# Two transformer blocks on one core: eight split chunks in output projections, row weights through GpSimd's queue, modulation on two engines

## The chip, the cores and the metric

The kernel runs on one core of a Trainium2 chip. The metric is the device time of one execution in microseconds (us). Times are medians of several runs; a profile is one execution more, with its own time.

## What is computed

Two transformer blocks in a row, on 512 tokens of width 1024, all in float32. Cut to what matters here:

```python
# first block: three residual steps, each  x = x + rms_norm(f(rms_norm(x, g_pre)), g_post)
mix = concat(fox_attention(...), chunked_rel_attention(...)) @ w_out
ca  = memory_cross_attention(h, m, w_mem_q, w_mem_kv, w_mem_o)
ff  = (silu(h @ w_gate) * (h @ w_up)) @ w_down

# second block, two layers (an mLSTM, then latent attention), each with
cond = silu(c)                                  # one vector of 1024
ada = cond @ ada_w[l] + ada_b[l]                # one row of 6 * 1024
sh1, sc1, g1, sh2, sc2, g2 = split(ada, 6)
h = rmsnorm(x, norm_g[l, 0]) * (1 + sc1) + sh1
y = mlstm_mixer(h, ...) if l == 0 else mla_mixer(h, ...)   # each ends in  @ w_out
x = x + g1 * rmsnorm(y, norm_g[l, 1])
h = rmsnorm(x, norm_g[l, 2]) * (1 + sc2) + sh2
x = x + g2 * rmsnorm(square(relu(h @ w1)) @ w2, norm_g[l, 3])
```

## The kernel before

Every float32 value that TensorE multiplies is held as two parts, high and low, and each product of 128 rows is three matmuls (L445, L446, L447: high by high, high by low, low by high). Weights are loaded raw on SP's queue (L421, four buffers), in chunks of up to 512 KB, and split on the chip: ScalarE writes the high part (L307, or L317 where a gain is multiplied in), VectorE the low part (L308, L318). At most `wcap` chunks are split and live at a time; `cap` sets that number for a stage: 4 for the first block's output projections, 5 for later ones. All split chunks and large activations lie in one pool of 14 buffers of 8 KB per partition.

Activations between stages are transposed and split too: `parts` makes the high part on ScalarE (L620) and the low part on VectorE (L621).

`out_lin` is an output projection (w_out, w_mem_o, a_w_out, b_w_out). It makes the first 512 columns for all four token tiles, and then, per token tile t, the other 512, followed by `boundary`. There the work of a token tile is a chain over four engines: ScalarE sums the squares of the product (L577), GpSimd makes the reciprocal root (`rstd`: L566, L560), VectorE multiplies by the gain row (L690) and adds to the residual (L641), ScalarE and GpSimd do the norm of the new residual (L577, L566, L560), ScalarE scales by it (L596), TensorE transposes (L606, in `put`), and `parts` follows (L620, L621). At three boundaries (before the mLSTM, and before the MLP of each layer of the second block) `put` also modulates: VectorE applies scale and shift to each of the eight 128x128 blocks of a token tile (L612), reading columns that `gcol` hands out.

These columns and the gain rows come from a background program, `ada`, a generator that is advanced one step at a time. `row_by` makes 512 numbers of a row: it loads eight pieces of the weights (L845, on SP's queue, two buffers `araw`), multiplies and adds them on VectorE (L841), folds the upper half of the partitions on the lower (L849), splits (L620, L621), sums over the partitions on TensorE (L858), finishes the row on VectorE (L871 or L875) and writes it to DRAM (L201). `row_cols` reads a whole row back as eight columns (L381), transposes it on TensorE (L385) and copies it (L387). Where the steps stand in the order of the work:

```python
    def step(self, cost):
        self.tick(cost)
        self.pace -= cost
        if self.pace < 0 and not self.quiet:
            self.pace = BUF["pacb" if self.late else "pace"]
            self.step_bg()

    def gcol(self, name):
        while name not in self.gcols:
            self.step_bg()
        return self.gcols[name]
```

`step` is called once per three matmuls with a cost of 0.65, so a step of the background is taken every 3 us of products (2.5 from the mLSTM on), and none in a boundary (`quiet`). Who calls `gcol` for columns that aren't there yet makes all missing steps on the spot. Instructions then go to the queues of the engines by a static order that the framework's scheduler works out at build time; each engine runs its queue in that order, and buffers of a pool are reused in it.

Of the kernel before, what the change touches and what calls it, by code (L numbers as in the profile page):

```python
# [10 lines left out]
F32 = mybir.dt.float32  # L11
# [3 lines left out]
AF = mybir.ActivationFunctionType  # L15
ALU = mybir.AluOpType
# [4 lines left out]
P = 128  # L21
# [3 lines left out]
KD = 8  # L25
# [5 lines left out]
D_FF = 2816  # L31
ALL = slice(0, S)

BUF = dict(s8=14, u2=17, row=2, raw=4, w0=4, w1=4, w2=4, w3=5, w4=5, w5=5, w6=5, w7=5, ps=8, pace=3, pacb=2.5, man=0, lag=3, lagx=3, lagm=3, half=1, quiet=1, xp=0, fp=2, r1=1.25, r1b=3.6, r1c=2.4, r2=1.6, r2b=2.6, rx=1.4, rm=0.6, pre=10, gl=3, pl=0, hb=300, hs=0, ha=0, sp=0, spq=1.3, sq=1, b1=1, b2=1, lc=7, mb=(6, 8, 6, 6, 6), mc=(4, 3, 4, 4, 4), st2=1, pr2=8, z1=4.5, z2=5, gt=3, rv=2, gs=1, rl=3, n1=4, ex=2, em=3, vg=1, sb=(8, 8, 6), mo=4, x1=2, g0=20, st=1, y1=0, y2=1, y3=0, ph=0, pq=0, fy=1, u1=6, s32=4, sm=60)

TWO_PI = 2.0 * np.pi

# [1 line left out]
def tt(t):  # L39
    return slice(t * P, (t + 1) * P)  # L40
# [98 lines left out]
class Net:  # L139
# [27 lines left out]
    def big(self, shape, dt=F32):  # L167
        return self.t("s8", shape, dt, BUF["s8"])

    def u2(self, shape=(P, S), dt=F32):  # L170
        if BUF["u1"] and int(np.prod(shape[1:])) <= 256:
            return self.t("u1", shape, dt, BUF["u1"])
        return self.t("u2", shape, dt, BUF["u2"])

    def row(self, n=DM):
        return self.t("row", [P, n], F32, BUF["row"])

    def sm(self, n=1, p=P, dt=F32):
        if n > 8:
            return self.t("sm32", [p, n], dt, BUF["s32"])  # L180
        return self.t("sm", [p, n], dt, BUF["sm"])
# [194 lines left out]
    def cols_steps(self, name, srcs, eng=None):  # L376
        n = sum(k for _, k in srcs)
        r = self.u2((n, P))
        o = 0
        for src, k in srcs:  # L380
            (eng or self.nc.gpsimd).dma_start(out=r[o:o + k, :], in_=src.rearrange("(k p) -> k p", p=P))  # L381
            o += k
        yield None
        ps = self.bank((P, n))
        self.nc.tensor.transpose(out=ps, in_=r, identity=self.ident[:n, :n])  # L385
        c = self.t(f"cols_{name}", [P, n], F32, 1)
        self.nc.vector.tensor_copy(out=c, in_=ps)  # L387
        yield c

    def gains(self):  # L390

        a = self.a
        names = (("out", "g_fox_out", 4), (None, "g_chunk_out", 4), ("mem", "g_mem_pre", 8), ("kvm", "g_mem_kv", 8),
                 ("ffn", "g_ffn_pre", 8), ("qlat", "b_q_latent_g_2", 3))
        srcs = [(a[m][0], n) for _, m, n in names]
        srcs += [(a["kv_latent_g_2"], 2), (a["a_head_g_2"][0].rearrange("h d -> (h d)"), 8)]
        steps = self.cols_steps("all", srcs)
        next(steps)
        yield
        gc = next(steps)  # L400
        o = 0
        for m, n in (("out", 8), ("mem", 8), ("kvm", 8), ("ffn", 8), ("qlat", 3), ("lat", 2), ("head", 8)):
            self.gcols[m] = gc[:, o:o + n]
            o += n
# [195 lines left out]
    def put(self, ys, h, k, t, mod=None):  # L600

        for y, cw in ys:
            n = cw // P
            ps = self.bank((P, n, P))
            for j in range(n):
                self.nc.tensor.transpose(out=ps[:, j, :], in_=y[:, tt(j)], identity=self.ident)  # L606
            hi, lo = h.blk(k, n, tt(t))
            if mod:
                g, sh = mod
                y = self.u2((P, n, P))  # L610
                for j in range(n):
                    self.nc.vector.tensor_scalar(out=y[:, j, :], in0=ps[:, j, :], scalar1=g[:, k + j:k + j + 1],  # L612
                                                 scalar2=sh[:, k + j:k + j + 1], op0=ALU.mult, op1=ALU.add)
                ps = y
            self.parts(hi, lo, ps)
            k += n
# [67 lines left out]

    def out_lin(self, w, h, g, nxt, first, gain=None):
        y0, s0 = [], []

        def by_gain(ps, c):
            y = self.u2()
            self.nc.vector.tensor_tensor(out=y, in0=ps, in1=g[:, c:c + S], op=ALU.mult)  # L690
            return y

        if self.started:
            wg, pss, k0 = self.started
            self.started = None
        else:
            wg, pss, k0 = self.weights(w, 0, KD, 0, S, gain=gain), [], 0
        for t in range(NT):
            ps = pss[t] if pss else self.bank()
            self.run(self.out_part(wg, ps, t, h, k0, KD))  # L700
            s0.append(self.meansq(ps, S, DM))
            y0.append(by_gain(ps, 0))
        wg = self.weights(w, 0, KD, S, S, gain=gain)

        def y_of(t):
            ps = self.bank()
            self.run(self.lin_N(ps, wg, t, h, last=t == NT - 1))
            ss = s0[t] + self.meansq(ps, S, DM)
            return (y0[t], by_gain(ps, S)), ss

        self.boundary(y_of, nxt, first)
# [115 lines left out]
    def row_by(self, i, c, ws, n, vec, b=None, gain=None, kind=0):  # L827

        nc, V = self.nc, self.nc.vector
        acc = self.u2((P, n))  # L830
        if b is not None:
            nc.gpsimd.memset(acc, 0.0)
            self.small(acc[0:1, :], b.rearrange("(o c) -> o c", o=1))
        yield
        raws = {}
        for k in range(0, KD + 2, 2):
            for j in (k, k + 1):
                if j == 2 and b is None:
                    V.tensor_scalar(out=acc, in0=raws.pop(0), scalar1=vec[:, 0:1], scalar2=None, op0=ALU.mult)
                elif j >= 2:  # L840
                    V.scalar_tensor_tensor(out=acc, in0=raws.pop(j - 2), scalar=vec[:, j - 2:j - 1], in1=acc,  # L841
                                           op0=ALU.mult, op1=ALU.add)
                if j < KD:
                    raws[j] = self.t("araw", [P, n], F32, 2)
                    nc.sync.dma_start(out=raws[j], in_=ws[:, j, :])  # L845
            yield
        if BUF["fy"]:
            h = P // 2
            (V if BUF["fy"] == 1 else nc.gpsimd).tensor_tensor(out=acc[0:h, :], in0=acc[0:h, :], in1=acc[h:P, :], op=ALU.add)  # L849
            hl = self.u2((P, n), F32R)  # L850
            for _ in range(BUF["y1"]):
                yield
            self.parts(hl[0:h, :], hl[h:P, :], acc[0:h, :])
            yield
            for _ in range(BUF["y2"]):
                yield
            ps = self.bank((P, n))
            nc.tensor.matmul(ps, lhsT=self.onesr, rhs=hl, start=True, stop=True)  # L858
        else:
            hi, lo = self.u2((P, n), F32R), self.u2((P, n), F32R)  # L860
            for _ in range(BUF["y1"]):
                yield
            self.parts(hi, lo, acc)
            yield
            for _ in range(BUF["y2"]):
                yield
            ps = self.bank((P, n))
            nc.tensor.matmul(ps, lhsT=self.onesr, rhs=hi, start=True, stop=False)
            nc.tensor.matmul(ps, lhsT=self.onesr, rhs=lo, start=False, stop=True)
        if gain is None:  # L870
            V.tensor_copy(out=acc[0:1, :], in_=ps[0:1, :])  # L871
        else:
            g = self.u2((1, n))
            self.small(g, gain.rearrange("(o c) -> o c", o=1))
            V.scalar_tensor_tensor(out=acc[0:1, :], in0=ps[0:1, :], scalar=1.0 if kind == 1 else 0.0,  # L875
                                   in1=g, op0=ALU.add, op1=ALU.mult)
        self.small(self.arow[i:i + 1, c:c + n], acc[0:1, :])
        if c or n < S:
            self.have.add(i)
        yield  # L880
# [1068 lines left out]
```

## Time and profile before

| | |
|---|---|
| runs | median 2008.97 us of 3 (2007.26 to 2010.29) |
| profiled execution | 2011.87 us |
| its span, first to last instruction | 2010.1 us |
| mean granted clock of TensorE | 0.987 |
| busy: TensorE, VectorE, ScalarE, GpSimd | 1947.1, 1283.3, 1022.9, 220.1 us |
| moved by DMA | 241.93 MB, 120 GB/s on average |

A row of the profile names the line of the kernel, the engine (PE is TensorE, PEld its weight loads, DVE VectorE, ACT ScalarE, POOL GpSimd, SP SyncE; a q behind a name is the engine's instruction queue), the operation, and out<-in by the program's names. An arrow in brackets names what ended the idle time ahead of the instruction.

### The profile page before, as it was taken

What the parts mean: (1) busy time and instruction counts of PE and PEld (TensorE: products, weight loads), DVE (VectorE), ACT (ScalarE), POOL (GpSimd) and SP (SyncE); (2) the same over time, 40 slices, a digit from 0 to 9 for tenths busy, and PEclk for the clock granted to TensorE, in tenths of its full rate; (3) what the DMA queues carried; (4) which work ended last, traced back from release to release, by engine and by line L of the source; (5) the groups of instructions that cost most, each with busy time, mean ns of one, the idle gap of its engine ahead of it and who ended that gap; (6) DMA issues with size and microseconds to landing.
All of it is one profiled execution on the core that took longest, in us unless ns stands there. A gap on an engine that the chain in (4) does not pass through costs nothing. (4 is left out here: it accounts for less than half of the span.)

```text
span 2010.1 us, 28210 instructions
## 1 busy us (share of the span) xinstructions
PE 1947.1 (97%) x10174; PEld 1647.7 (82%) x10174; DVE 1283.3 (64%) x2565; ACT 1022.9 (51%) x2236; POOL 220.1 (11%) x463
## 2 busy tenths in 40 slices
PE   8999998999999999998998999999999989999998
PEld 5888987878888888777887888887888879989987
DVE  5756654756657675667776556566669745757666
ACT  6767775537244333545545442442565645545444
POOL 1331111001000100111112000000120012000000
PEclk9999999999999999999998999999999999999999
DMA  6322342433446463235342446455243212233322
GB/s 211 90 79 67 113 139 72 144 109 97 146 147 199 153 193 110 76 111 157 102 134 88 137 148 209 147 181 184 66 129 120 70 51 71 82 106 118 99 75 83
DMA packets 190988, 241.93 MB, mean 120 GB/s; under 512 B 20107, under 2 KB 119584, under 8 KB 190848
## 3 DMA queue, kind: packets, MB, share of 16 engines
q1 hardware_dynamic: 185264, 232.15, 36.7%
q0 software_dynamic: 5584, 7.98, 1.5%
q8 instruction: 80, 1.31, 0.3%
q14 instruction: 60, 0.49, 0.1%
HBM read 237.88 MB, written 2.20 MB: 119 GB/s over the span
## 5 line engine op out<-in xcount | busy, mean ns | idle before, releaser
L445 PE MATMUL ps<-s,s 128*128 128x512 f32 (+4 forms) x2452 | 935.8, 384 | 33.1 <-ACT s L620 33.1
L446 PE MATMUL ps<-s,s 128*128 128x512 f32 (+5 forms) x2452 | 927.2, 379 | 1.5 <-DVE s L621 1.5
L447 PE MATMUL ps<-s,s 128*128 128x512 f32 (+5 forms) x2452 | 926.2, 379 | 2.4 <-DVE s L621 2.4
L445 PEld LDWEIGHTS ps<-s,s 128*128 128x128 f32 (+1 forms) x2452 | 464.4, 190 | 119.7 <-ACT s L620 36.1
L447 PEld LDWEIGHTS ps<-s,s 128*128 128x128 f32 (+2 forms) x2452 | 463.9, 189 | 92.7 <-DVE s L621 3.9
L446 PEld LDWEIGHTS ps<-s,s 128*128 128x128 f32 (+2 forms) x2452 | 465.0, 190 | 87.5 <-DVE s L621 2.7
L307 ACT ACTIVATE s<-raw 128x512 fp32r<-128x512 f32 x329 | 185.3, 621 | 179.2 <-PE ps L447 118.4
L308 DVE TENSOR_TENSOR s<-raw,s 128x512 fp32r<-128x512 f32 x329 | 212.0, 686 | 66.7 <-ACT s L307 65.2
L841 DVE SCALAR_TENSOR_TENSOR u<-araw,cond,u 128x512 f32<-128x512 f32 x224 | 168.2, 751 | 134.7 <-DMA araw<-in_ada_w 108.0
L317 ACT ACTIVATE s<-raw,cols_all 128x256 fp32r<-128x256 f32 (+1 forms) x305 | 143.1, 545 | 39.5 <-issue 19.1
L318 DVE SCALAR_TENSOR_TENSOR s<-raw,cols_all,s 128x256 fp32r<-128x256 f32 (+1 forms) x305 | 147.2, 537 | 16.4 <-ACT s L317 14.8
L508 PEld LDWEIGHTS ps<-s,s 128*128 128x128 f32 x1092 | 130.0, 189 | 1.0
L508 PE MATMUL ps<-s,s 128*128 128x256 f32 x1092 | 130.3, 280 | 0.0
L621 DVE TENSOR_TENSOR s<-u,s 128x512 fp32r<-128x512 f32 x118 | 80.6, 691 | 71.8 <-ACT s L620 67.2
L620 ACT ACTIVATE s<-u 128x512 fp32r<-128x512 f32 x118 | 73.5, 627 | 74.5 <-DVE u L1392 58.4
L201 POOL DMA_DIRECT2D arow<-u x30 | 14.7, 489 | 707.1 <-DVE u L875 401.7
L621 DVE TENSOR_TENSOR s<-ps,s 128x512 fp32r<-128x512 f32 (+3 forms) x100 | 59.4, 605 | 44.1 <-ACT s L620 43.2
L1427 ACT ACTIVATE u<-ps 128x512 f32<-128x512 f32 x38 | 22.6, 596 | 104.2 <-PE ps L447 104.1
L1332 DVE TENSOR_TENSOR u<-ps,u 128x512 f32<-128x512 f32 x80 | 53.5, 683 | 29.8 <-PE ps L447 29.4
L620 ACT ACTIVATE s<-ps 128x512 fp32r<-128x512 f32 (+3 forms) x100 | 51.5, 527 | 38.8 <-PE ps L606 12.4
L566 POOL TENSOR_SCALAR sm<-sm,sm 128x1 f32<-128x1 f32 x34 | 11.3, 332 | 495.4 <-ACT junk L577 494.8
L318 DVE SCALAR_TENSOR_TENSOR s<-raw,cols_mix,s 128x128 fp32r<-128x128 f32 (+2 forms) x152 | 52.4, 400 | 9.7 <-ACT s L317 9.4
(257 smaller groups left out, 1976.1 us busy)
## 6 DMA issues: line engine op xcount, KB each, us to landing
raw<-in_mlp_w SPq DMA_DIRECT2D x128, 512.0 KB, 4.0
araw<-in_ada_w SPq DMA_DIRECT2D x192, 256.0 KB, 3.0
raw<-in_w_gate_up SPq DMA_DIRECT2D x44, 512.0 KB, 4.2
raw<-in_w_in SPq DMA_DIRECT2D x24, 512.0 KB, 4.7
raw<-in_a_w_in SPq DMA_DIRECT2D x24, 512.0 KB, 3.8
raw<-in_w_down SPq DMA_DIRECT2D x22, 512.0 KB, 4.1
raw<-in_w_mem_kv SPq DMA_DIRECT2D x16, 512.0 KB, 3.5
araw<-in_kv_ada_w SPq DMA_DIRECT2D x32, 256.0 KB, 2.7
```

The costliest lines, as they stand in the source:

```text
L307: A.activation(hi[:, sl, cl], src[:, sl, cl], AF.Copy)
L308: f.tensor_tensor(out=lo[:, sl, cl], in0=src[:, sl, cl], in1=hi[:, sl, cl].bitcast(F32), op=ALU.subtract)
L317: A.activation(hi[:, i, :], src[:, i, :], AF.Copy, scale=g)
L318: V.scalar_tensor_tensor(out=lo[:, i, :], in0=src[:, i, :], scalar=g, in1=hi[:, i, :].bitcast(F32), op0=ALU.mult, op1=ALU.subtract)
L445: self.nc.tensor.matmul(ps, lhsT=ah, rhs=bh, start=first and i == 0, stop=False)
L446: self.nc.tensor.matmul(ps, lhsT=ah, rhs=bl, start=False, stop=False)
L447: self.nc.tensor.matmul(ps, lhsT=al, rhs=bh, start=False, stop=last and i == n - 1)
L508: nc.tensor.matmul(ps, lhsT=l[:, k, :], rhs=m[:, k, :], start=first and k == e == 0, stop=k == 3 and e == 2, skip_group_check=True)
L620: self.nc.scalar.activation(hi, x, AF.Copy)
L621: self.nc.vector.tensor_tensor(out=lo, in0=x, in1=hi.bitcast(F32), op=ALU.subtract)
L841: V.scalar_tensor_tensor(out=acc, in0=raws.pop(j - 2), scalar=vec[:, j - 2:j - 1], in1=acc, op0=ALU.mult, op1=ALU.add)
L1332: V.tensor_tensor(out=y, in0=ps, in1=y, op=ALU.add)
```

## The change

`out_lin` sets `wcap` to 8 for its stage. The pieces of row weights are loaded on GpSimd's queue instead of SP's, into four buffers instead of two, and each is multiplied two steps after its load instead of one, so that `row_by` has one step more (10 instead of 9). `cols_steps` waits three steps instead of one between the read-back and the transpose, so that `row_cols` has two more (4 instead of 2). In `put`, blocks 0 and 1 of every four are modulated on VectorE and blocks 2 and 3 on ScalarE. The pool of 2 KB buffers has 15 instead of 17.

```diff
-BUF = dict(s8=14, u2=17, ...
+BUF = dict(s8=14, u2=15, ..., oc=8, ar=4, ...
@@ cols_steps
-        yield None
+        for _ in range(3):
+            yield None
@@ gains
-        gc = next(steps)
+        for gc in steps:
+            pass
@@ put
-                    self.nc.vector.tensor_scalar(out=y[:, j, :], in0=ps[:, j, :], scalar1=g[:, k + j:k + j + 1],
-                                                 scalar2=sh[:, k + j:k + j + 1], op0=ALU.mult, op1=ALU.add)
+                    gj, sj = (c[:, k + j:k + j + 1] for c in (g, sh))
+                    if j < 2:
+                        self.nc.vector.tensor_scalar(out=y[:, j, :], in0=ps[:, j, :], scalar1=gj, scalar2=sj,
+                                                     op0=ALU.mult, op1=ALU.add)
+                    else:
+                        self.nc.scalar.activation(y[:, j, :], ps[:, j, :], AF.Identity, scale=gj, bias=sj)
@@ out_lin
         y0, s0 = [], []
+        self.cap(BUF["oc"], True)
@@ row_by
-        for k in range(0, KD + 2, 2):
+        for k in range(0, KD + 4, 2):
+            for j in (k - 4, k - 3):
+                if j == 0 and b is None:
+                    V.tensor_scalar(out=acc, in0=raws.pop(0), scalar1=vec[:, 0:1], scalar2=None, op0=ALU.mult)
+                elif j >= 0:
+                    V.scalar_tensor_tensor(out=acc, in0=raws.pop(j), scalar=vec[:, j:j + 1], in1=acc,
+                                           op0=ALU.mult, op1=ALU.add)
             for j in (k, k + 1):
-                if j == 2 and b is None:
-                    V.tensor_scalar(out=acc, in0=raws.pop(0), scalar1=vec[:, 0:1], scalar2=None, op0=ALU.mult)
-                elif j >= 2:
-                    V.scalar_tensor_tensor(out=acc, in0=raws.pop(j - 2), scalar=vec[:, j - 2:j - 1], in1=acc,
-                                           op0=ALU.mult, op1=ALU.add)
                 if j < KD:
-                    raws[j] = self.t("araw", [P, n], F32, 2)
-                    nc.sync.dma_start(out=raws[j], in_=ws[:, j, :])
+                    raws[j] = self.t("araw", [P, n], F32, BUF["ar"])
+                    nc.gpsimd.dma_start(out=raws[j], in_=ws[:, j, :])
             yield
```

How the order of the instructions changes is shown at three places. The changed kernel is a few lines longer, so its lines have other numbers: L386, L447 to L449, L598, L608, L626, L647, L848, L853, L857, L866, L883 and L579 are there what L385, L445 to L447, L596, L606, L620 (L627 for L621), L641, L841, L845, L849, L858, L875 and L577 are before.

TensorE at the boundary after b_w_out, before: ps_15370 is the second half of the product for token tile 1, ps_15417 for tile 2, ps_15490 for tile 3, and L606 transposes tile 0.

```order
L446 MATMUL ps_15370<-s_2956_15267,s_2878_14948 128x512
L447 MATMUL ps_15370<-s_2956_15267,s_2879_14949 128x512
L445 MATMUL ps_15417<-s_2869_14919,s_2717_14411 128x512
L446 MATMUL ps_15417<-s_2869_14919,s_2717_14411 128x512
...
L447 MATMUL ps_15417<-s_2956_15267,s_2879_14949 128x512
L606 MATMUL ps_15447<-ident_66,u_2987_15400 128x128 x4
L606 MATMUL ps_15460<-ident_66,u_2988_15402 128x128 x4
L445 MATMUL ps_15490<-s_2869_14919,s_2717_14411 128x512
```

The same place in the changed kernel: ps_15233 is the product for tile 1, ps_15367 for tile 2.

```order
L448 MATMUL ps_15233<-s_2903_15109,s_2825_14786 128x512
L449 MATMUL ps_15233<-s_2903_15109,s_2826_14787 128x512
L866 MATMUL ps_15302<-u_2953_15299,onesr_78 128x512
L866 MATMUL ps_15339<-u_2965_15336,onesr_78 128x512
L386 MATMUL ps_15347<-ident_66,u_2968_15345 128x8
L447 MATMUL ps_15367<-s_2816_14757,s_2663_14250 128x512
L608 MATMUL ps_15397<-ident_66,u_2940_15263 128x128 x4
L608 MATMUL ps_15410<-ident_66,u_2941_15265 128x128 x4
L448 MATMUL ps_15367<-s_2816_14757,s_2663_14250 128x512
```

Both partition sums of row 10 and the transpose of its columns now stand between the two products; before, the two sums stand about 960 and 590 instructions further ahead.

VectorE at the same place in the changed kernel, from the residual of tile 1 on (six products of each half of the row left out):

```order
L647 SCALAR_TENSOR_TENSOR x_9_90<-u_2939_15261,sm_15356,x_9_90 128x512
L848 SCALAR_TENSOR_TENSOR u_2944_15271<-araw_15274,cond_4066,u_2944_15271 128x512
...
L848 SCALAR_TENSOR_TENSOR u_2944_15271<-araw_15292,cond_4066,u_2944_15271 128x512
L857 TENSOR_TENSOR u_2944_15271<-u_2944_15271 64x512
L627 TENSOR_TENSOR u_2953_15299<-u_2944_15271,u_2953_15299 64x512
L883 SCALAR_TENSOR_TENSOR u_2944_15271<-ps_15302,u_2955_15304 1x512
L848 SCALAR_TENSOR_TENSOR u_2956_15308<-araw_15311,cond_4066,u_2956_15308 128x512
...
L848 SCALAR_TENSOR_TENSOR u_2956_15308<-araw_15329,cond_4066,u_2956_15308 128x512
L857 TENSOR_TENSOR u_2956_15308<-u_2956_15308 64x512
L627 TENSOR_TENSOR u_2965_15336<-u_2956_15308,u_2965_15336 64x512
L883 SCALAR_TENSOR_TENSOR u_2956_15308<-ps_15339,u_2967_15341 1x512
```

Before, the residual of tile 1 is followed by L690 of tile 2 and the modulation of tile 0, and no row product stands in the boundary.

ScalarE at the boundary after the first out_lin, before: s_800 and s_803 are the transposed activation, L317 splits the weights of the next product.

```order
L596 ACTIVATE u_806_3682<-x_9_90,sm_3630 128x512
L620 ACTIVATE s_803_3676<-ps_3671 128x4x128
L317 ACTIVATE s_814_3704<-raw_3496,cols_all_1926 128x256 x4
L317 ACTIVATE s_815_3713<-raw_3509,cols_all_1926 128x256 x2
L577 ACTIVATE junk_3691,sm_3690<-x_10_91 128x1024
L317 ACTIVATE s_815_3713<-raw_3509,cols_all_1926 128x256 x2
L317 ACTIVATE s_816_3722<-raw_3522,cols_all_1926 128x256 x4
L317 ACTIVATE s_817_3731<-raw_3535,cols_all_1926 128x256 x4
L620 ACTIVATE s_800_3667<-ps_3741 128x4x128
```

And in the changed kernel, where s_808 and s_811 are that activation:

```order
L598 ACTIVATE u_814_3726<-x_9_90,sm_3674 128x512
L626 ACTIVATE s_808_3711<-ps_3706 128x4x128
L579 ACTIVATE junk_3735,sm_3734<-x_10_91 128x1024
L626 ACTIVATE s_811_3720<-ps_3715 128x4x128
L317 ACTIVATE s_822_3748<-raw_3528,cols_all_1926 128x256 x4
L626 ACTIVATE s_808_3711<-ps_3785 128x4x128
```

Of the 16 splits that stood between the two token tiles' L620, four are left there.

## Rows read from the trace of the kernel before

**Rows 1.** The page, first part: busy us (share of the span) and instructions of each engine.

```profile
PE 1947.1 (97%) x10174; PEld 1647.7 (82%) x10174; DVE 1283.3 (64%) x2565; ACT 1022.9 (51%) x2236; POOL 220.1 (11%) x463
```

**Rows 2.** Waits of TensorE over the span: line, releaser, us, times, longest.

```profile
PE ps L445 <- ACT s L620: 33.1, 10, 8.3
PE ps L858 <- DVE u L621: 5.3, 1, 5.3
...
PE ps L385 <- DMA u<-arow: 3.1, 1, 3.1
```

**Rows 3.** Timeline, boundary after b_w_out, TensorE: start us, us, engine, line, operation.

```profile
1637.67 0.39 PE L445 MATMUL ps<-s,s 128*128 128x512 f32 x1
```

**Rows 4.** Timeline of VectorE: columns "10" ready, and the boundary after b_w_out.

```profile
1502.10 0.17 DVE L387 COPY cols<-ps 128x8 f32<-128x8 f32 x1 [0.30 <-PE ps L385]
...
1636.52 1.41 DVE L641 SCALAR_TENSOR_TENSOR x<-u,sm,x 128x512 f32<-128x512 f32 x2 [0.37 <-POOL sm L560]
...
1641.21 1.42 DVE L641 SCALAR_TENSOR_TENSOR x<-u,sm,x 128x512 f32<-128x512 f32 x2 [0.59 <-POOL sm L560]
...
1645.23 2.64 DVE L612 TENSOR_SCALAR u<-ps,cols,cols 128x128 f32<-128x128 f32 x8
```

**Rows 5.** VectorE's row products L841: a wait of theirs, us and times.

```profile
  DMA araw<-in_ada_w: 108.0, 83
```

**Rows 6.** Timeline of 903 to 920 us: SP's queue, VectorE, ScalarE, TensorE.

```profile
903.90 9.73 SPq L845 DMA_DIRECT2D araw<-in_kv_ada_w  x5
...
912.53 0.75 DVE L841 SCALAR_TENSOR_TENSOR u<-araw,cond,u 128x512 f32<-128x512 f32 x1
913.20 1.89 DVE L308 TENSOR_TENSOR s<-raw,s 128x512 fp32r<-128x512 f32 x3
915.11 0.69 DVE L849 TENSOR_TENSOR u<-u 64x512 f32<-64x512 f32 x1
...
915.83 0.63 ACT L620 ACTIVATE u<-u 64x512 fp32r<-64x512 f32 x1 [2.11 <-DVE u L849]
...
918.89 0.77 PE L858 MATMUL ps<-u,onesr 128*128 128x512 f32 x1 [5.25 <-DVE u L621]
```

**Rows 7.** The chain that ended last, at 1387 to 1394 us: start us, us, what.

```profile
1387.74 0.49 DMA arow<-u
...
1390.49 2.98 DMA u<-arow
...
1393.52 0.22 PE ps L385
```

**Rows 8.** DMA issues (KB each, median us to landing), and the spread of negG's landings.

```profile
araw<-in_ada_w SPq DMA_DIRECT2D x192, 256.0 KB, 3.0
...
u<-negG POOLq DMA_DIRECT2D x8, 256.0 KB, 3.7
...
arow<-u POOLq DMA_DIRECT2D x28, 2.0 KB, 2.0
...
u<-arow POOLq DMA_DIRECT2D x10, 4.0 KB, 1.7
...
DMA to landing us min/median/max: 1.8/3.7/5.8
```

**Rows 9.** Timeline of ScalarE at the boundary after the first out_lin.

```profile
330.50 2.50 ACT L317 ACTIVATE s<-raw,cols_all 128x256 fp32r<-128x256 f32 x6
...
333.94 4.09 ACT L317 ACTIVATE s<-raw,cols_all 128x256 fp32r<-128x256 f32 x10
337.93 0.58 ACT L620 ACTIVATE s<-ps 128x512 fp32r<-128x512 f32 x1
```

**Rows 10.** ScalarE: splits after b_w_out, and a form of L620 (ns min/median/max).

```profile
1648.44 4.26 ACT L307 ACTIVATE s<-raw 128x512 fp32r<-128x512 f32 x8
...
L620 ACT ACTIVATE u<-ps x20: 257/590/608, 1488.5 to 1585.7; 128x512 fp32r<-128x512 f32 x16, 128x128 fp32r<-128x128 f32 x4
```

**Rows 11.** Timeline of the start: TensorE's second matmul, tile 1's norm on GpSimd.

```profile
9.61 0.63 PE L446 MATMUL ps<-s,s 128*128 128x512 f32 x1
...
13.50 0.82 POOL L593 TENSOR_SCALAR u<-x,sm 128x512 f32<-128x512 f32 x1
```

**Rows 12.** Busy us by engine in one stretch; PEclk is the granted clock (1.00 is full).

```profile
916.00:923.00 7.00, 4.11 (x10) 3.31 (x11) 6.56 (x9) 3.60 (x9) 1.66 (x3) 0.53 0.46 144
```

More of the change, by code (lines that the diff above doesn't have):

```diff
@@ L32 @@
 ALL = slice(0, S)
-BUF = dict(s8=14, u2=17, row=2, raw=4, w0=4, w1=4, w2=4, w3=5, w4=5, w5=5, w6=5, w7=5, ps=8, pace=3, pacb=2.5, man=0, lag=3, lagx=3, lagm=3, half=1, quiet=1, xp=0, fp=2, r1=1.25, r1b=3.6, r1c=2.4, r2=1.6, r2b=2.6, rx=1.4, rm=0.6, pre=10, gl=3, pl=0, hb=300, hs=0, ha=0, sp=0, spq=1.3, sq=1, b1=1, b2=1, lc=7, mb=(6, 8, 6, 6, 6), mc=(4, 3, 4, 4, 4), st2=1, pr2=8, z1=4.5, z2=5, gt=3, rv=2, gs=1, rl=3, n1=4, ex=2, em=3, vg=1, sb=(8, 8, 6), mo=4, x1=2, g0=20, st=1, y1=0, y2=1, y3=0, ph=0, pq=0, fy=1, u1=6, s32=4, sm=60)
+BUF = dict(s8=14, u2=15, row=2, raw=4, w0=4, w1=4, w2=4, w3=5, w4=5, w5=5, w6=5, w7=5, ps=8, pace=3, pacb=2.5, man=0, lag=3, lagx=3, lagm=3, half=1, quiet=1, xp=0, fp=2, r1=1.25, r1b=3.6, r1c=2.4, r2=1.6, r2b=2.6, rx=1.4, rm=0.6, pre=10, gl=3, pl=0, hb=300, hs=0, ha=0, sp=0, spq=1.3, sq=1, b1=1, b2=1, lc=7, oc=8, ar=4, mb=(6, 8, 6, 6, 6), mc=(4, 3, 4, 4, 4), st2=1, pr2=8, z1=4.5, z2=5, gt=3, rv=2, gs=1, rl=3, n1=4, ex=2, em=3, vg=1, sb=(8, 8, 6), mo=4, x1=2, g0=20, st=1, y1=0, y2=1, y3=0, ph=0, pq=0, fy=1, u1=6, s32=4, sm=60)
 TWO_PI = 2.0 * np.pi
```

## The prediction

> **What bounds the kernel now.** I read the busy shares first: TensorE works 97% of the span [rows 1], so no arithmetic is taken away by this change and the time can only move through the pauses of TensorE and through its clock. The list of what TensorE waited for comes next [rows 2]: 33.1 us in ten waits of L445 for ScalarE's L620 (the high parts of an activation after a boundary, 8.3 us the longest), one wait of 5.3 us of L858, one of 3.1 us of L385 for a row read back from DRAM. All pauses together are 63 us (2010.1 less 1947.1). After a pause the granted clock falls too: in the stretch after the wait of L858 it was 0.53, the lower of the two levels [rows 12], and TensorE's work took twice as long there. So a pause costs its length plus some microseconds. Then, for the places where the change moves instructions, I read the timelines and the order.
>
> **The background grows by 50 steps, and one row comes late: the largest term.** row_by yields 10 times instead of 9 (30 calls: 30 steps), row_cols 4 times instead of 2 (10 calls: 20 steps). Steps are handed out at a fixed pace of TensorE's work (2.5 us in the second half), so 50 steps are at least 125 us of products, and more on the clock, since attention and boundaries hand out none. Before, the columns "10" (the scale of the boundary after b_w_out) were finished at 1502.1 us, and that boundary's first residual additions come some 135 us later [rows 4]: no room is left. The order shows the result: nxt's gcol("10") now forces the row inside the boundary. On TensorE, in order, the two L858 of row 10 and its L385 stand between token tile 1's product and tile 2's product; on VectorE all 16 products of row 10 stand behind tile 1's L641. Nothing that TensorE could do instead stands ahead of them.
>
> Its length, by rows: TensorE is free when tile 1's product ends, at 1637.7, and tile 1's L641 ends at 1641.21 + 1.42 = 1642.6 [rows 3, 4]: 4.9 us. Sixteen products L841 start 0.67 apart where nothing holds them (912.53 to 913.20 [rows 6]): 10.7 us. Two tails (L849 0.69, L620 0.63, then L621 and L875, which I take as long as L849, and L858 at full clock, half of its 0.77 [rows 6]) are about 3.1 each: 6.2 us. Writing the row to DRAM and reading it back took 5.8 us from issue to L385 in the one place where TensorE waited for it [rows 7]; with the medians of landing, 2.0 and 1.7, it is about 4 [rows 8]. The floor, with every weight already on the chip, is 4.9 + 10.7 + 6.2 + 4 = 26 us. The weights aren't all there: four buffers hold four of the 16 loads, so rounds two and four wait for a landing. A landing takes 3.0 us at the median from SP's queue; the nearest rows for 256 KB from GpSimd's queue are negG's, 1.8 at least, 3.7 at the median, 5.8 at most [rows 8]. A round of products covers 2.7 us of it, which leaves some 1.7 for each of two rounds, and a little for GpSimd's own instructions between (two issues, a memset, tile 1's rstd). I take 30 us (negG's median; between 26 and 36, the end with landings of 5.8 in every round). TensorE restarts at the lower clock and loses about 2.5 us more, as after L858's wait (4.1 us busy in that stretch at half speed [rows 12]). **+32.5 us, between 27 and 39.** The 7 us pause that stands behind this boundary today stays.
>
> **Row products two steps behind their loads.** Before, VectorE stood at L841 until the weight had landed, 108.0 us in 83 waits for in_ada_w alone [rows 5]. That hurts TensorE in one place: at 903.9 SP needed 9.73 us for five loads, VectorE's products and so L849, L621 and L858 came late, and TensorE idled 5.25 us [rows 6]. With four buffers and two steps of distance the wait goes: −5.25, and −2.1 of half clock: **−7.4** (−7.4 to −2, if half the pause stays). The rule of the Trainium skill, "DMA: Bandwidth & Descriptors", section "Issuing engines are not separate DMA queues", says that the queues of all engines feed the same 16 DMA engines and that a second queue saves only issue time. The trace speaks differently for this place: SP's queue lost its time to waiting for a buffer, not to issuing, with raw weights queued behind. By the rule alone this term would be near 0 and the sum 7 us higher.
>
> **Columns two more steps behind their read-back.** L385's wait of 3.1 us [rows 2, 7] goes, with about 1.7 of low clock after it: **−4.8** (−4.8 to 0).
>
> **Eight chunks in out_lin.** At the first out_lin ScalarE's order changes: today 16 splits L317 (6, then 10 in 4.09 us) stand ahead of tile 1's L620 at 337.93 [rows 9]; after, four do. Twelve splits at 0.41 are 4.9 us on ScalarE, the pause there is 3.6 us and its low clock some 1.7: **−4.5** (−6 to −2.5). At the memory, a_w_out and b_w_out boundaries the splits of the next weights that stand ahead of tile 1's norm and L620 are as many as before (16, 8 and 8; the eight take 4.26 us [rows 10]): they are of later chunks, which costs ScalarE the same. **0**: those pauses stay.
>
> **Half the modulation on ScalarE.** 48 of 96 L612 move. Eight take VectorE 2.64 us per token tile [rows 4], so VectorE gains 1.3. ScalarE gains four of 128x128 from PSUM, for which the nearest row is the shortest L620, 0.26 [rows 10]: some 1.1 us per token tile, on the engine whose eight splits, norm and L620 are the chain at this boundary. For tile 0 it fills a wait of ScalarE for L612; for tile 1 it is on the path, less VectorE's gain. **+0.5** at each of three boundaries, **+1.5** (0 to 4.5, with all of it on the path at each).
>
> **The start.** GpSimd now issues four weight loads (1 MB) ahead of the first rstd, and tile 1's transposes stand behind TensorE's second matmul instead of its 22nd. Today tile 1's norm is ready no earlier than 13.50 + 0.82 on GpSimd [rows 11], TensorE's second matmul starts at 9.6: a wait of some 4 us, part of which returns as a shorter wait for tile 3 at 25 us. **+3.3** (0 to 6, if tile 1's input lands later as well).
>
> **mLSTM.** GpSimd's queue now has the weight loads among its 256 KB loads of negG; a load that waits for a buffer holds what is behind it. No row prices it; I take **0**, within one landing: ±3.
>
> **The sum.** 32.5 − 7.4 − 4.8 − 4.5 + 1.5 + 3.3 = +20.6 us on the profiled execution, 2011.87 (a span of 2010.1 and 1.8 around it): 2032.5. That execution is 2.9 above the median of the runs, 2008.97, so I expect 2029.5. All low ends together give 2015, all high ends 2057; a measurement of this kernel can tell about 0.2%, 4 us.
>
> **Rivals.**
> A, not slower: the boundaries shrink instead. The mechanism is ScalarE at the boundaries: with eight chunks held, the splits are done during the previous product, and the ten waits for L620 go. Price: up to some 28 of the 33.1 us [rows 2] and about 12 of low clock behind them instead of my −4.5 + 1.5; 2029.5 − 37 = 1993. It breaks even where the boundaries give 24 us. Against it: the order keeps the splits ahead of L620 at all but one, and the forced row's 26 us has no way round in TensorE's order. Chance 0.13, for all degrees of it.
> B, GpSimd's queue is slow under VectorE's load: landings at negG's worst, 5.8 [rows 8], so the forced row costs 36, the pause at 913 stays, and GpSimd's rstd waits behind loads in mLSTM: 2029.5 + 6 + 7 + 3 = 2045. The Trainium skill has a rule for it, "SBUF — State Buffer", 'The "DVE blocks DMA" trap (SWDGE)': while VectorE runs certain two-port operations, GpSimd can't write its descriptors and its transfers stall. The spread of negG's landings allows it, no row shows it. Chance 0.17.
> C, the change does not do what it says: the eight chunks find no room in the pool even at the first out_lin. Then −4.5 falls away: 2034. Chance 0.1.
> My forecast, a net loss by the forced row: 0.6.
>
> **Numbers.** Range 2006 to 2046: it takes in forecast, B and C, and half of A. Slower 0.85 (all but A and a small part of the forecast's low end), same 0.07, faster 0.08.
>
> **What would show it.** TensorE's waits should have new rows, L858 for VectorE's L621 and L385 for the row's read-back, of some 30 us together near 1640 to 1670, with the clock low behind them; no wait at 913 and none of L385 at 1390; the pause at 335 under 2 us, those at 465, 1078 and 1651 as long as now, and a wait of L606 near 10 us. If TensorE has no wait above 10 us at the boundary after b_w_out, the prediction is wrong.

## The result and the profile after

The changed kernel takes 2039.08 us at the median of four runs (2038.71 to 2042.21), the kernel before 2009.63 in the same series (2007.26 to 2011.11): a ratio of 1.0151, with a 95% interval of 1.0134 to 1.0169. Slower, as forecast, and inside the range. The profiled execution took 2038.71 us, 26.8 more than that of before; +20.6 was forecast.

The waits of TensorE in the changed kernel (line, releaser: us, times, longest) answer to [rows 2]:

```profile
PE ps L447 <- ACT s L626: 32.9, 9, 9.8
PE ps L866 <- DVE u L627: 25.6, 2, 14.7
PE ps L608 <- DVE u L595: 6.7, 1, 6.7
PE ps L386 <- DMA u<-arow: 6.1, 1, 6.1
```

L866 is the partition sum of a row (L858 before). It waits 25.6 us in two waits, and L386, the transpose of the row's columns, 6.1. The timeline of TensorE shows where (the background's matmuls alone; the value in brackets is the idle time ahead):

```profile
1644.19 0.77 PE L866 MATMUL ps<-u,onesr 128*128 128x512 f32 x1 [14.69 <-DVE u L627]
1655.92 0.79 PE L866 MATMUL ps<-u,onesr 128*128 128x512 f32 x1 [10.96 <-DVE u L627]
1662.81 0.27 PE L386 MATMUL ps<-ident,u 8*128 8x8 f32 x1 [6.10 <-DMA u<-arow]
```

31.75 us in a row, at the boundary after b_w_out. VectorE in the same stretch:

```profile
1631.84 1.42 DVE L647 SCALAR_TENSOR_TENSOR x<-u,sm,x 128x512 f32<-128x512 f32 x2 [0.83 <-POOL sm L562]
1633.54 3.12 DVE L848 SCALAR_TENSOR_TENSOR u<-araw,cond,u 128x512 f32<-128x512 f32 x4 [0.28 <-DMA u<-in_ada_b]
1637.51 0.75 DVE L848 SCALAR_TENSOR_TENSOR u<-araw,cond,u 128x512 f32<-128x512 f32 x1 [0.86 <-DMA araw<-in_ada_w]
1639.06 0.75 DVE L848 SCALAR_TENSOR_TENSOR u<-araw,cond,u 128x512 f32<-128x512 f32 x1 [0.79 <-DMA araw<-in_ada_w]
1640.40 1.54 DVE L848 SCALAR_TENSOR_TENSOR u<-araw,cond,u 128x512 f32<-128x512 f32 x2 [0.60 <-DMA araw<-in_ada_w]
...
1645.56 0.68 DVE L883 SCALAR_TENSOR_TENSOR u<-ps,u 1x512 f32<-1x512 f32 x1 [1.51 <-DMA u<-in_norm_g]
1646.16 3.09 DVE L848 SCALAR_TENSOR_TENSOR u<-araw,cond,u 128x512 f32<-128x512 f32 x4
1650.15 0.75 DVE L848 SCALAR_TENSOR_TENSOR u<-araw,cond,u 128x512 f32<-128x512 f32 x1 [0.90 <-DMA araw<-in_ada_w]
...
1657.97 0.68 DVE L883 SCALAR_TENSOR_TENSOR u<-ps,u 1x512 f32<-1x512 f32 x1 [2.11 <-DMA u<-in_norm_g]
```

This is the row as the prediction laid it out: four products whose weights are there, four that wait for landings, a tail, and the same again. Two small waits in it were not foreseen: VectorE stands 1.51 and 2.11 us ahead of L883. The partition sum takes 0.77 and 0.79 us of them; the rest, some 0.6 and 1.3 us, is a gain row of 2 KB that GpSimd loads behind the row weights.

Where the 26.8 us came from is told by the distance between the two traces. I took TensorE's matmuls in the order in which they start, without those of the background, and subtracted the start times of equal places (after less before; the time is that of before):

```
at us        after less before
35           +6.5     start
352          +6.6     boundary after the first projection
735          +9.7     cross attention, first half of the gated MLP
859          +6.6     boundary before the mLSTM
925          -0.7     mLSTM
1206         -1.4     a_w_out and its boundary
1398         -6.1     MLP of the first layer
1628         -8.7     latent attention, b_w_out
1645        +26.8     boundary after b_w_out; unchanged from here to the end
```

So up to the boundary after b_w_out the changed kernel is ahead by 8.7 us, and it loses 35.5 there.

### The profile page after: what moved, and what is told of

Same layout as the page of the kernel before. It is cut to its first block, busy times and chain, and to the rows that moved or that the text cites. A ratio compares the mean times of both kernels' runs of the same rounds, so it can differ in the third digit from the quotient of the medians.

```text
span 2036.9 us, 28332 instructions
## 1 busy us (share of the span) xinstructions
PE 1943.1 (95%) x10174; PEld 1643.7 (81%) x10174; DVE 1279.7 (63%) x2517; ACT 1036.7 (51%) x2282; POOL 345.4 (17%) x703
## 3 DMA queue, kind: packets, MB, share of 16 engines
q0 software_dynamic: 24400, 69.60, 11.3%
## 5 line engine op out<-in xcount | busy, mean ns | idle before, releaser
L447 PE MATMUL ps<-s,s 128*128 128x512 f32 (+4 forms) x2452 | 934.6, 383 | 32.9 <-ACT s L626 32.9
L449 PE MATMUL ps<-s,s 128*128 128x512 f32 (+5 forms) x2452 | 922.9, 378 | 0.6 <-DVE s L627 0.6
L447 PEld LDWEIGHTS ps<-s,s 128*128 128x128 f32 (+1 forms) x2452 | 463.1, 189 | 119.7 <-ACT s L626 35.9
L449 PEld LDWEIGHTS ps<-s,s 128*128 128x128 f32 (+2 forms) x2452 | 462.3, 189 | 89.6 <-DVE s L627 1.2
L307 ACT ACTIVATE s<-raw 128x512 fp32r<-128x512 f32 x329 | 185.9, 622 | 205.0 <-PE ps L449 161.6
L848 DVE SCALAR_TENSOR_TENSOR u<-araw,cond,u 128x512 f32<-128x512 f32 x224 | 168.1, 750 | 40.0 <-DMA araw<-in_ada_w 23.5
L317 ACT ACTIVATE s<-raw,cols_all 128x256 fp32r<-128x256 f32 (+1 forms) x305 | 143.2, 546 | 63.1 <-PE ps L449 34.2
L853 POOL DMA_DIRECT2D araw<-in_ada_w x192 | 104.8, 546 | 296.5 <-DVE u L848 273.6
L627 DVE TENSOR_TENSOR s<-u,s 128x512 fp32r<-128x512 f32 x118 | 85.3, 737 | 104.1 <-ACT s L626 83.8
L626 ACT ACTIVATE s<-u 128x512 fp32r<-128x512 f32 x118 | 72.1, 629 | 58.4 <-DVE u L1400 25.8
L627 DVE TENSOR_TENSOR s<-ps,s 128x512 fp32r<-128x512 f32 (+3 forms) x100 | 58.9, 605 | 40.7 <-ACT s L626 39.6
L626 ACT ACTIVATE s<-ps 128x512 fp32r<-128x512 f32 (+3 forms) x100 | 50.7, 525 | 27.4 <-PE ps L1292 11.7
```

What stands on the lines that cost most here:

```text
L307: A.activation(hi[:, sl, cl], src[:, sl, cl], AF.Copy)
L317: A.activation(hi[:, i, :], src[:, i, :], AF.Copy, scale=g)
L447: self.nc.tensor.matmul(ps, lhsT=ah, rhs=bh, start=first and i == 0, stop=False)
L449: self.nc.tensor.matmul(ps, lhsT=al, rhs=bh, start=False, stop=last and i == n - 1)
L626: self.nc.scalar.activation(hi, x, AF.Copy)
L627: self.nc.vector.tensor_tensor(out=lo, in0=x, in1=hi.bitcast(F32), op=ALU.subtract)
```

## The experiments

My theory: the loss is the row of the background that is forced inside that boundary because the background has 50 steps more. Rivals: (1) GpSimd's queue is the slower way for the 62 MB of row weights that it now moves (69.60 MB in the page's row of its queue, 7.98 before); (2) the eight chunks or the modulation on ScalarE cost. Each run below has its ratio to the kernel before in its own series. All runs of the changed kernel keep the smaller pool of 2 KB buffers, the fast ones too, so the pool is not the loss.

**e2_rows_only, e3_eight_only, e4_mod_only: one part at a time.** The first takes these two edits out of the changed kernel, the others put one of them alone into the kernel before:

```diff
-        self.cap(BUF["oc"], True)          # e2: removed; e3: added alone (8 chunks)
-                    if j < 2: ...          # e2: L612 for all blocks again; e4: this split alone
```

> Only the part of the change on the background (loads on GpSimd's queue, four buffers, products two steps later, columns two steps later, 15 small buffers); the projections keep four or five chunks and VectorE does all the modulation. Theory: all of the loss is in this part: the forced row stays, the gain at the transition to the mLSTM (some 3 us) may go with the modulation: 2036 to 2042. Rival 2: most of the loss goes, under 2020.

> The kernel before with eight chunks in the output projections and nothing else. Theory: the first projection's boundary loses about what it gains, the others have as many splits ahead of L620 as before: within 3 us of before, 2006 to 2012. Rival A of the prediction (eight chunks shorten the boundaries): 1995 or less.

> The kernel before with half of the modulation on ScalarE and nothing else. Theory: VectorE's gain and ScalarE's load nearly cancel at the boundaries after a_w_out and b_w_out, and the transition to the mLSTM, where ScalarE has no splits ahead, gains up to 3 us: 2004 to 2010. The prediction's own value was a loss of 1.5 (0 to 4.5): 2009 to 2014.

Measured: 2043.15 us, ratio 1.0168 (1.0153 to 1.0183), for the background's part alone, 1 us above what I expected; 2008.49, 0.9989 (0.9979 to 1.0000), for eight chunks alone; 2005.56, 0.9981 (0.9972 to 0.9990), for the modulation alone. Rival 2 falls: the whole loss lies in the background's part. The kernel with the modulation alone gains 0.2%, but not all by the modulation: of the 7 us that its trace is ahead at the end, 2.7 stand at the boundary before the mLSTM and 3.8 near 1394 us, where a read-back came sooner. Rival A of the prediction (eight chunks shorten the boundaries) falls too. In e2_rows_only the same three waits stand at the boundary after b_w_out:

```profile
PE ps L861 <- DVE u L623: 26.5, 2, 15.4
PE ps L386 <- DMA u<-arow: 6.1, 1, 6.1
```

**e5_sync_queue: the queue alone.**

```diff
-                    nc.gpsimd.dma_start(out=raws[j], in_=ws[:, j, :])
+                    nc.sync.dma_start(out=raws[j], in_=ws[:, j, :])
```

> The whole change, but the weights of the row products are loaded on SP's queue again (four buffers, products two steps later as in the change). Theory: the steps are the same and row 10 is forced at the same place; its loads land some 0.4 us sooner and GpSimd has less to do there, 2 to 4 us of the 31.8; the start goes back to that of before (5 to 6 us): 2028 to 2034. Rival 1 (GpSimd's queue and its landings are the loss): 2020 or less.

Measured: 2030.64, ratio 1.0100 (1.0084 to 1.0116). Its waits of TensorE:

```profile
PE ps L866 <- DVE u L627: 23.9, 2, 13.8
PE ps L386 <- DMA u<-arow: 5.9, 1, 5.9
...
PE ps L608 <- DVE u L595: 1.9, 1, 1.9
```

The forced row is 2 us shorter, and the wait of the start (6.7 in the changed kernel) is back at 1.9. Each in its own series, this kernel loses 20 us and the changed one 29: rival 1 explains some 9 of the 29 us, most of them at the start (at 35 us this trace stands at −2.0, the changed one at +6.5), not the rest. The wait of L858 in the mLSTM does not come back. VectorE's products waited 134.8 us for row weights before, 24.6 in the changed kernel and 16.7 here: two steps of distance with four buffers freed VectorE, not the queue. That this alone took TensorE's wait away is not shown. The extra steps also moved the background, and the sum that stands there now is an earlier one, the 11th of the program instead of the 13th, whose L627 had ended 10 us before (changed kernel, timelines of VectorE and TensorE):

```profile
913.35 0.69 DVE L627 TENSOR_TENSOR u<-u,u 64x512 fp32r<-64x512 f32 x1 [0.70 <-ACT u L626]
923.75 0.39 PE L866 MATMUL ps<-u,onesr 128*128 128x512 f32 x1
```

**e1_pace, e8_late_pace, e12_before_pace: time for the extra steps.** The number that sets how often a background step is taken is changed, in the changed kernel twice and once in the kernel before:

```diff
-pace=3, pacb=2.5
+pace=2.55, pacb=2.1     # e1_pace
+pace=3, pacb=1.9        # e8_late_pace; e12_before_pace (in the kernel before)
```

> The whole change, but the background takes a step every 2.55 us of products (2.1 in the second half) instead of 3 (2.5), so that its 50 extra steps fit and row 10 is done before the boundary after b_w_out. Theory (the loss is the row forced inside that boundary): its three waits of 31.8 us and the low clock behind them go, the other stages stay as in the changed kernel: about 35 us less than 2039, 2002 to 2006, faster than before by 3 to 7 us. Rival 1 (the queue of GpSimd with its slower landings is what costs): the loads are the same and come denser, no more than 10 us come back, 2029 or more. Rival 2 (eight chunks and the modulation on ScalarE cost): nothing of theirs changes, 2035 or more.

> The whole change, with a background step every third group of three matmuls from the mLSTM on (1.95 us of products) instead of every fourth (2.6); the first half keeps its pace, which the run before this did not (2.55 there also made every fifth group every fourth). Theory: nothing moves up to 1040 us, row 10 is ready before the boundary after b_w_out, and the 35.5 us that the changed kernel loses there shrink to 1 or 2; denser row products on VectorE cost up to 3 elsewhere: 2003 to 2009. Rival 1: denser loads on GpSimd's queue hold its other work, 2015 or more.

> The kernel before with the faster second half alone. Theory: its background was never late, so the pace by itself gives nothing; its products still wait for their loads, now closer together: within 4 us of before or up to 4 slower, 2006 to 2014. Rival (the gain of the runs with the faster half is the pace itself): 2003 or less.

e1_pace: 2015.85, ratio 1.0029 (1.0017 to 1.0040). No wait above 10 us is left at the boundary after b_w_out and that stage loses 1 us instead of 35, but I expected 2002 to 2006. The edit was not what I had written: `step` counts groups of 0.65 and starts afresh at each step, so 3 means five groups (3.25 us of products), and 2.55, 2.5 and 2.1 all mean four (2.6). The second half was unchanged and the first half ran denser. With it another row came to the mLSTM's gate computation, and L866 waited there again (TensorE's waits):

```profile
PE ps L866 <- DVE u L627: 3.5, 1, 3.5
```

It is not the wait of [rows 6]: no weight is late. ScalarE's half of the split ended at 901.7 us, and VectorE's half, L627, started at 903.08, behind the gate computation in VectorE's queue. Between 853 and 925 us this run gains 1.4 us where the changed kernel gains 8.7. e8_late_pace makes the first half as in the change and every third group a step in the second: 2006.55, ratio 0.9985 (0.9972 to 0.9998), as expected; 32.5 us of the changed kernel are gone with one number, and all loads still go through GpSimd's queue. That settles the theory against rival 1, but for its 9 us.

e12_before_pace came out worse than expected: 2017.57, ratio 1.0042 (1.0030 to 1.0055). The pace is no gain of its own: with one step between read-back and transpose, denser steps make TensorE wait for the row's landing twice (below), while e8_late_pace, with the same pace and three steps, has one such wait of 0.5 us:

```profile
PE ps L385 <- DMA u<-arow: 5.5, 2, 3.6
```

**e6_cols_one: 30 extra steps instead of 50.**

```diff
-        for _ in range(3):
-            yield None
+        yield None
```

> The whole change, but the columns are transposed one step after their read-back as before, so that the background has 30 steps more instead of 50. In this kernel's order all 16 products of row 10 stand ahead of the boundary after b_w_out, and only the second partition sum, the row's write and its read-back stand inside it. Theory (the loss is what stands of the row inside the boundary, step by step): the waits of 14.7 and 11.0 us go, that of some 6 to 8 us for write and read-back stays: 24 to 26 us less than the changed kernel, 2012 to 2017. A read-back one step ahead may bring the wait of 3 us near 1390 back (up to 4 more). Rival (20 of 50 steps, in proportion): 14 less, 2024 to 2028.

Measured: 2035.20, ratio 1.0132 (1.0117 to 1.0148). Missed by 18 us, and the trace says why. The boundary after b_w_out did what the theory says in kind: its waits are 4.1 (L865, which I had put at nothing) and 7.6 us instead of 31.75, and the stage loses 15 us instead of 35.5. But the background stands elsewhere: the columns of row 0 take two steps less, and products of the next row fell into the boundary after the memory attention. That boundary costs some 6 us more than in the changed kernel. TensorE waits twice there, where the changed kernel has one wait of 5.0 us (timeline, idle time in brackets):

```profile
476.17 1.97 PE L607 MATMUL ps<-ident,u 128*128 128x128 f32 x8 [5.13 <-ACT u L597]
481.49 0.80 PE L446 MATMUL ps<-s,s 128*128 128x256 f32 x2 [3.36 <-ACT s L625]
```

GpSimd's queue reads:

```profile
457.91 0.55 POOL L852 DMA_DIRECT2D araw<-in_ada_w  x1 [1.43 <-DVE u L847]
458.53 0.74 POOL L567 TENSOR_SCALAR sm<-sm 128x1 f32<-128x1 f32 x1
459.33 0.59 POOL L852 DMA_DIRECT2D araw<-in_ada_w  x1
459.95 0.58 POOL L561 TENSOR_TENSOR sm<-sm,mhalf 128x1 f32<-128x1 f32 x1
...
461.17 0.61 POOL L567 TENSOR_SCALAR sm<-sm,sm 128x1 f32<-128x1 f32 x1
...
468.95 0.56 POOL L561 TENSOR_TENSOR sm<-sm,mhalf 128x1 f32<-128x1 f32 x1
```

Two reciprocal roots (L567, L561) stand between row weights, one of which waited for VectorE to free a buffer. That is rival B's mechanism, GpSimd's queue holding a reciprocal root, but it is not what TensorE waited for. Tile 1's root, the last row above, was there at 469.5 us, and ScalarE began tile 1's norm L597 only at 475.40, behind sixteen splits:

```profile
468.45 3.29 ACT L317 ACTIVATE s<-raw,cols_all 128x256 fp32r<-128x256 f32 x8
...
472.21 3.29 ACT L317 ACTIVATE s<-raw,cols_all 128x256 fp32r<-128x256 f32 x8
475.40 1.33 ACT L597 ACTIVATE u<-x,sm 128x512 f32<-128x512 f32 x2
```

In the changed kernel the same norm stands ahead of the splits:

```profile
468.35 1.34 ACT L598 ACTIVATE u<-x,sm 128x512 f32<-128x512 f32 x2
469.58 4.90 ACT L317 ACTIVATE s<-raw,cols_all 128x256 fp32r<-128x256 f32 x12
```

So the moved row cost its time mainly through ScalarE's order in the static schedule. The roots between row weights came late too (ScalarE stood 0.75 us for tile 0's, 0.27 in the changed kernel), but TensorE's wait did not end with them. With it, and with a wait in the mLSTM like e1_pace's (3.5 us at 907), e6_cols_one is 10.6 us behind the kernel before at 925 us, where the changed kernel is 0.7 ahead. Another 4.4 us against the changed kernel, between 925 and 1628, are not explained here. What a background step costs depends on what it meets.

**e9_late_start, e10_late_sync, e11_no_eight: towards a better kernel.** All three have the second half's pace of e8_late_pace. The first also holds the first four row weights until the condition vector exists, the second loads them on SP's queue, the third is the second without eight chunks.

```diff
+                    if i == 0 and c == 0 and j < BUF["ar"]:                       # e9
+                        V.tensor_copy(out=raws[j][:, 0:1], in_=vec[:, 0:1])
-                    nc.gpsimd.dma_start(out=raws[j], in_=ws[:, j, :])             # e10, e11
+                    nc.sync.dma_start(out=raws[j], in_=ws[:, j, :])
-        self.cap(BUF["oc"], True)                                                 # e11
```

> As the run with the faster second half, and the first four row weights may only be loaded once the condition vector is there (one column of each buffer is written from it first), so that they no longer compete with the inputs at the start; tile 1's transposes stand behind the 22nd matmul again. Theory: the 6.4 us of the start come back and nothing else changes: 5 to 7 below the run with the faster second half alone, 1997 to 2003, faster than before by 0.3 to 0.6%. Rival (the start is slow for another reason, the order alone or the smaller pool): less than 2 us come back.

> The faster second half with the row weights on SP's queue (four buffers, two steps). Theory: the distance of two steps is what frees VectorE, the queue matters little; the start is that of before, and the wait of L858 in the mLSTM (5.3 us before) goes as in the change: 1996 to 2003. Rival (the gain at 913 us comes from GpSimd's own queue, since SP's holds raw weights behind a blocked load): the wait of some 5 us and its low clock stay, 2003 to 2010.

> The faster second half and SP's queue as in the run that had both, but the output projections keep four or five chunks. Theory: eight chunks gain nothing at any boundary but lose some 4 to 5 us between 340 and 740 us (a wait of L448 for VectorE of 2.9 and one of L1292 for ScalarE of 1.5 that the kernel before does not have): 1994 to 1998. Rival (the eight chunks help): above 2001.

e9_late_start: 2005.40, ratio 0.9971 (0.9960 to 0.9983); I expected 1997 to 2003. It is only 1 us below e8_late_pace at the median, which would be the rival, while their two profiles differ by 7.6 us, 4.2 of them at the start (TensorE's wait for L595 is 1.8 instead of 5.5). Their runs overlap (2000.2 to 2008.5 against 2002.8 to 2013.1), so what the start alone is worth stays open, between 1 and 7 us. e10_late_sync: 2000.31, ratio 0.9950 (0.9934 to 0.9967), as expected. e11_no_eight: 2000.30, ratio 0.9958 (0.9945 to 0.9970); I expected 1994 to 1998, and eight chunks turn out to cost nothing over the whole kernel, nor to gain. e10_late_sync, the change on SP's queue with time for its extra steps, is faster than both kernels, by 0.5% and, from one series to the other, 1.9%. Its waits:

```profile
PE ps L447 <- ACT s L626: 28.6, 8, 9.7
PE ps L386 <- DMA u<-in_g_mix_pre: 5.3, 1, 5.3
PE ps L448 <- DVE s L627: 3.3, 2, 2.9
PE ps L1804 <- DVE u L1813: 3.2, 1, 3.2
```

There is no L866 among them any more.

## Why the prediction was right, term by term

**The forced row, +32.5 (27 to 39): 35.5.** From the end of tile 1's product to the restart 33.6 us were measured for the 30 taken: 31.75 us of waits and 1.8 of the background's three matmuls. With the low clock after it the stage lost 35.5. Row weights landed 3.1 us after their issue at the median in this stretch (2.8 to 3.8; negG's 3.7 was taken), which is why the middle of the range held. What was left out is the small gain row in GpSimd's queue (some 0.6 and 1.3 us). The granted clock was 0.53 in the stretch, the lower level, and the work after it started there (the first L447 takes 0.80 us, those from 1666 us on 0.40):

```profile
1629.50:1663.10 33.60, 1.85 (x5) 0.84 (x4) 21.52 (x30) 4.31 (x8) 18.69 (x35) 0.53 0.45 136
1663.10:1671.20 8.10, 8.10 (x34) 6.81 (x35) 3.30 (x6) 0.02 (x1) 2.14 (x4) 0.83 0.68 217
```

(stretch, its us, busy us of TensorE, its weight loads, VectorE, ScalarE and GpSimd, granted clock, DMA share, GB/s.)

**Row products two steps behind, −7.4: −7.2** between 859 and 925 us, with no wait of L858 left. The size is right and the way only in part shown: VectorE's waits for row weights went, but another sum stands at the place than before (e5_sync_queue above), and e1_pace has a wait of 3.5 us there with the same buffers and distance. So part of this may be luck of the place. The weighing of the rule of the Trainium skill ("DMA: Bandwidth & Descriptors", section "Issuing engines are not separate DMA queues") went half each way. e5_sync_queue shows that the second queue as such was not needed, as the rule has it, but the term came all the same.

**Columns, −4.8: −4.7** between 1206 and 1398 us. Part of this is luck: in e3_eight_only and e4_mod_only, whose background is that of the kernel before, the same wait is 1.9 and 0.9 us instead of 3.1 [rows 7]. And it is the columns "9" that wait at 1393.5 us before; in the changed kernel they come at 1623.75, without a wait, and another row stands near 1394. That the distance matters is shown by all runs together: with one step, waits of this kind outside the forced row are 0.9 to 5.5 us, with three steps at most 0.6.

**Eight chunks, −4.5: the step that failed.** The boundary gained nothing (+6.5 at 35 us, +6.6 at 352), and the stages behind it lost 3. e3_eight_only, eight chunks alone, shows the same in its trace: 0.5 us lost up to 352, 3.0 more up to 735. Over the whole kernel it is no slower than before all the same (2.7 us come back near 1394, as in e4_mod_only). The 12 splits did leave tile 1's L620, but eight of them now stand ahead of tile 2's norm, as ScalarE's timeline shows:

```profile
343.72 3.30 ACT L317 ACTIVATE s<-raw,cols_all 128x256 fp32r<-128x256 f32 x8
346.91 1.33 ACT L598 ACTIVATE u<-x,sm 128x512 f32<-128x512 f32 x2
...
435.75 3.38 ACT L317 ACTIVATE s<-raw,cols_all 128x256 fp32r<-128x256 f32 x8 [0.85 <-DMA raw<-in_w_gate_up]
439.03 0.41 ACT L1278 ACTIVATE u<-ps 128x128 f32<-128x128 f32 x2
```

TensorE's transposes waited 2.75 us for that L598. And in the cross attention eight splits stand ahead of an L1278 for which TensorE waits 1.6 us. I followed the moved splits out of one wait and not into the next.

**Modulation, +1.5: about −3.** Before the mLSTM the boundary gained 3.1 us (+9.7 to +6.6), and e4_mod_only gains 2.7 there: VectorE came last at that place (L447 waited 1.5 us for L621, which is gone), so that what it no longer does is worth its time. e3_eight_only, without the modulation, gains 1.3 there too, so the two shares are not told apart. The reason that I gave in that run's expectation, no splits on ScalarE there, is wrong: seven L307 stand ahead of the norm as elsewhere. At a_w_out the pause grew from 8.3 to 9.8 us and a wait of 1.1 behind it went, at b_w_out it grew from 7.2 to 7.7: there the two engines' shares nearly cancel. Four blocks take ScalarE 1.50 us, where 1.1 was taken (ScalarE at a_w_out; VectorE's four take 1.36 at b_w_out, timelines):

```profile
1071.63 1.50 ACT L619 ACTIVATE u<-ps,cols,cols 128x128 f32<-128x128 f32 x4 [0.23 <-DVE u L616]
...
1672.51 1.36 DVE L616 TENSOR_SCALAR u<-ps,cols,cols 128x128 f32<-128x128 f32 x4
```

**The start, +3.3 (0 to 6): +6.5.** Both causes named were there, and the second more than I took: tile 1's input landed later behind the four row weights. ScalarE's first sum of squares of tile 1, before and after:

```profile
9.80 0.63 ACT L577 ACTIVATE junk<-x 128x512 bf16<-128x512 f32 x1 [0.35 <-DMA x<-in_x]
```

```profile
13.47 0.63 ACT L579 ACTIVATE junk<-x 128x512 bf16<-128x512 f32 x1 [3.25 <-DMA x<-in_x]
```

**The sum, +20.6: +26.8.** Eight chunks were some 7.6 us too low and the modulation some 4.6 too high; that these two errors have opposite signs is luck. And 2.6 us were gained between 1398 and 1628 by no term of the sum; the cause is open.

**Of the rivals,** A is refuted by e3_eight_only. C's mechanism, no room for the chunks, is refuted by the order of the splits just shown, though what it forecast, −4.5 falling away, came true in another way. B did not decide: the landings in the forced row took 3.8 us at most, and the pause at 913 went. A root held in GpSimd's queue was seen in e6_cols_one, but TensorE did not wait for it. The rule of the Trainium skill on GpSimd's descriptors ("SBUF — State Buffer", 'The "DVE blocks DMA" trap (SWDGE)') is not needed: in the forced row, between VectorE's products, the row weights landed in 3.1 us at the median.

## What to carry to other kernels

When a pipeline step is added to work that is handed out at a fixed pace, count all steps to each deadline: here 50 steps of nothing but distance made one row late, and its whole latency, 32 us, fell on the critical path, while the waits that the distance was meant to remove were gone. A counter that is set afresh at each step rounds its pace up to whole units, so that some settings are the same program. And where a static order is worked out for the whole program, a step moved at one place can move other work at another: in e6_cols_one two steps less put sixteen splits ahead of one norm. Compare the order of all engines there before a queue is blamed.

## What I had not expected

GpSimd's small instructions are slower next to its DMA issues: in e6_cols_one the two forms of L567 take 0.74 and 0.61 us between row weights, and 0.22 (at 468.65 us) and 0.30 us (at 454 us) with none just ahead. And a small shift decides whether TensorE waits for a read-back: 3.1, 1.9 and 0.9 us at the same instruction in three kernels with the same background. Each is one execution, so what is chance in it is not shown.
